# The half-GLU of the S5 branch, moved from ahead of the merge to between two branches of it

## The chip, the cores and the metric

One core of a Trainium2 chip runs the whole step in one launch. The metric is the device time in microseconds, the median of three runs. Engines: TensorE (PE; its weight loads are PEld), VectorE (DVE), ScalarE (ACT), GpSimd (POOL) and SyncE (SP, which here only issues DMAs). Each engine runs its own instructions in program order and waits on semaphores for the others.

## The reference

One inference step of a two-layer decoder trunk with model width 1024, on 1024 prompt tokens and 64 sample tokens, 1088 columns (T) in all, in float32. A layer is

```
h = rmsnorm(x);  proj = h @ w_in          # columns for four mixers, their gates z, and 4 x 1024 merge gates
y_a = conv branch          y_c = HGRN2 branch          y_d = GLA branch
sg  = gelu(y_s)                           # y_s: output of the S5 state space scan
y_b = sg * sigmoid(sg @ w_glu + b_glu) * silu(s_z)
p_b = y_b @ w_branch[b]                   # for each of the four branches, 512 -> 1024
merged = sum_b sigmoid(g_b) * p_b
x = x + merged @ w_out
```

After the second layer comes a last RMSNorm. The states of the four mixers are outputs too.

## The kernel before

Activations lie feature-major, 128 features x 1088 columns to a tile (`[128, T]`), in a pool of `NBIG = 38` such tiles. A float32 matmul is done as three passes over rounded parts: a tile is split into hi (a copy to float32r on ScalarE) and lo (a subtraction on VectorE), and hi*hi, lo*hi and hi*lo are summed in PSUM (`split`, line 1851; for weights `prep`, line 295: `whi` and `wlo`). A unit (`unit`, line 353) makes 128 output features: two halves of 544 columns, each over 4 or 8 tiles of the contraction with 3 passes and 2 matmuls of 272 columns; a unit over 4 tiles has 48 matmuls. It has three PSUM tiles (`mm`), evacuated by the function `out` that the caller gives.

All engine queues are written by one Python program, so the order of its calls is the order on each engine. Two devices put side work among a unit's matmuls. `self.defer` is a list of small jobs, of which `step` takes one at every second k of a unit (four steps to a unit over 4 tiles, eight over 8). And four lanes of generators (`rec` for the recurrences of HGRN2 and GLA, `s5l` and `tabs` for S5, `aux`) are advanced by `pump`: a bookkeeper (`Book`, line 93) holds estimated times of each engine, and a lane's next stage is written when its inputs and PSUM banks should be ready, enough tiles are free (`fits`) and VectorE is not more than `BACKLOG` = 12 us behind. `make_room` (line 234) writes lane stages at once when the pool is nearly full, `drain` (line 228) until a lane is empty.

A layer runs paired projections first (`PAIRED`), then `ORDER`: single gate units m20 to m31, the HGRN2 heads H0 to H3, the GLA pairs G0 and G1, and U. A gate unit stores sigmoid(g) to DRAM (`gsc`); silu(s_z) is in `szs`, the S5 scan's output in `vsc`, and y of each branch in `ysc`. During the last unit of G1 (line 1835) `glu_begin` loads the four S5 tiles (`yv`) and defers GELU and split of each (`xh`, `xl`). U (`glu`, line 1696) first loads y of branch 0, then for each of four units: sigmoid from PSUM (`glu`), times silu(s_z) (`sz`, loaded a unit ahead), the sum of xh and xl on POOL as the other factor, the product (`yb`, its columns reordered), and the store to `ysc`.

`merge` (line 1861) then runs 32 units, 8 for each branch in the order 0, 2, 1, 3. A unit's result is multiplied by its gate tile (`g`, loaded two units ahead with `gate`) and added to `merged` (`mg`). At d = 5 of a branch the next branch's y is loaded and its splits are deferred; ahead of branch 3 the lanes `rec` and `aux` are drained. Weights come through a ring of `RAWS` = 6 raw tiles (`w_dma`, line 273), loaded by SyncE in the order of `make_plan`. A raw load waits on SyncE until the tile that had its place has been split.

All instructions are recorded by a helper and have line 84, so the rows are told apart by their tiles.

Of the kernel before, what the change touches and what calls it, by code (L numbers as in the profile page):

```python
# [9 lines left out]
F32 = mybir.dt.float32  # L10
# [19 lines left out]

PAIRED = 'A0 M0 A1 M1 A2 M2 A3 M3 Z0 M4 Z1 M5 M6 M7 M8'
EARLY = 'm18 m19'
ORDER = 'm20 m21 m22 m23 m24 m25 m26 m27 m28 m29 m30 m31 H0 H1 H2 H3 G0 G1 U'
BRANCHES = (0, 2, 1, 3)

# [113 lines left out]
class Trunk:  # L151
# [121 lines left out]
    def w_dma(self, i):  # L273
        if i >= len(self.plan) or i in self.loaded:
            return
        self.loaded.add(i)
        self.nraw += 1
        src, M, perm = self.plan[i]
        raw = self.wp.tile([128, 4, 128], F32, tag="wraw", name=self.nm("wraw"), bufs=RAWS)
        if perm == 2:  # L280
            for k in range(4):
                self.nc.sync.dma_start(raw[:, k, :], src[128 * k:128 * k + 128, :].rearrange("(g p) m -> p g m", p=16))
        else:
            r = raw[:] if M < 256 else raw[:].rearrange("p a b -> p (a b)").rearrange("p (k m) -> p k m", m=M)
            self.nc.sync.dma_start(r, src.rearrange("(k p) m -> p k m", p=128))
        self.raws[i] = raw
# [8 lines left out]
    def prep(self, j):  # L295

        if j >= len(self.seq) or j in self.done:
            return
        self.done.add(j)
        nc = self.nc  # L300
        e, p = self.seq[j]
        perm = self.plan[e][2]
        drop = []
        for i in range(e, e + (1 if p is None else 4)):
            self.w_dma(i)
        if p is None:
            src = self.raws[e]
            drop = [e]
        else:

            a11, a21, a22, a12 = (self.raws.get(e + i) for i in range(4))
            new = lambda: self.wp.tile([128, 4, 128], F32, tag="wsum", name=self.nm("wsum"), bufs=2)
            if p == 0:
                src = a11
            elif p == 1:
                s1 = new()
                src = new()
                self.sums_[e] = s1, src
                nc.vector.tensor_add(s1[:], a21[:], a22[:])
                nc.vector.tensor_sub(src[:], s1[:], a11[:])  # L320
            elif p == 2:
                src = a12
            elif p == 3:
                src = self.sums_[e][0]
            elif p == 4:
                src = a21
                nc.vector.tensor_sub(a21[:], a11[:], a21[:])
                drop = [e, e + 1]
            elif p == 5:
                src = self.sums_.pop(e)[1]  # L330
                nc.vector.tensor_sub(src[:], a12[:], src[:])
                drop = [e + 3]
            else:
                src = a22
                drop = [e + 2]
        hi = self.wp.tile([128, 4, 128], F32R, tag="whi", name=self.nm("whi"), bufs=4)
        lo = self.wp.tile([128, 4, 128], F32R, tag="wlo", name=self.nm("wlo"), bufs=4)
        h, lv, r = hi[:], lo[:], src[:]
        if perm:
            h, lv = (x.rearrange("q k (p g) -> q k g p", g=8) for x in (h, lv))  # L340
            r = r.rearrange("q k (g p) -> q k g p", g=8)
        nc.scalar.activation(h, r, AF.Copy)
        nc.vector.tensor_sub(lv, r, h.bitcast(F32))
        for i in drop:
            self.raws.pop(i)
            self.nraw -= 1
        self.ws[j] = (hi, lo)
# [257 lines left out]
    def make_plan(self):  # L605
# [14 lines left out]
        for l in range(DEPTH):  # L620
# [13 lines left out]
            for op in ORDER.split():  # L634
                t, j = op[0], int(op[1:] or 0)
                names = []
                if t == "H":
                    names = [("c_i", j // 2, 256)] if j % 2 == 0 else []
                    names += [(n, j, 128) for n in ("c_f", "c_q", "c_z")]
                elif t == "m":  # L640
                    names = [(f"g{j // 8}", j % 8, 128)]
                elif t == "G":
                    names = [("d_q", j, 128), ("d_k", j, 128)] + ([("d_v", j, 256)] if j else [])
                    names += [("d_z", 2 * j, 128), ("d_z", 2 * j + 1, 128)]
                else:
                    add([(self.a["w_glu"][l][:, 128 * i:128 * i + 128], 128, 2) for i in range(4)])
                for n, i, M in names:
                    add(self.w_src(l, n, i, M))
            for br in BRANCHES:
                add([(self.a["w_branch"][l, br][:, 128 * d:128 * d + 128], 128, 0) for d in range(8)])  # L650

    def proj(self, l, name, j, out, last=False):
        self.unit(8, self.h, out, last)
# [1013 lines left out]
    def glu_begin(self, l):  # L1667
# [1 line left out]
        nc = self.nc  # L1669
        self.drain(self.tabs)  # L1670
        self.drain(self.s5l)
        sg = self.sg = [None] * 4

        def load(j):
            t = self.big([128, T], name="yv")
            nc.sync.dma_start(t.rearrange("q (t c) -> q t c", t=8),
                              self.vsc[l][j][:].rearrange("(t p) (g c) -> (p g) t c", t=8, g=8))
            sg[j] = t

        def act(j):  # L1680
            t = sg[j]
            nc.scalar.activation(t, t, AF.Gelu_apprx_tanh)
            hi = self.big([128, T], F32R, "xh")
            lo = self.big([128, T], F32R, "xl")
            nc.scalar.activation(hi, t, AF.Copy)
            nc.vector.tensor_sub(lo, t, hi.bitcast(F32))
            self.free(t)
            sg[j] = (hi, lo)

        for j in range(4):  # L1690
            load(j)
        self.defer += [lambda: None] * YLAG
        for j in range(4):
            self.defer.append(lambda j=j: act(j))

    def glu(self, l):
        nc = self.nc
        sg = self.sg

        def gate(j):  # L1700
            sz = self.big([128, T], name="sz")
            nc.sync.dma_start(sz, self.szs[l][j][:])
            return sz

        nxt = gate(0)
        while self.defer:
            self.defer.pop(0)()
        self.y = self.load_y(l, BRANCHES[0])
        self.defer += [lambda: None] * 4 + [lambda j=j: self.split(self.y, j) for j in range(4)]
        for j in range(4):  # L1710
            sz, nxt = nxt, gate(j + 1) if j < 3 else None
            g = self.big([128, T], name="glu")
            c = 40 + 4 * l + j
            self.unit(4, sg, self.evac(g, AF.Sigmoid, bias=self.cols[:, c:c + 1]))
            nc.vector.tensor_mul(g, g, sz)
            yt = self.big([128, T], name="yb")
            yn = yt.rearrange("p (c s) -> p s c", s=8)
            nc.gpsimd.tensor_add(sz, sg[j][0].bitcast(F32), sg[j][1].bitcast(F32))
            v3 = lambda t: t.rearrange("p (s c) -> p s c", s=8)
            nc.vector.tensor_mul(yn, v3(sz), v3(g))  # L1720
            nc.sync.dma_start(self.ysc[l][1][128 * j:128 * j + 128, :].rearrange("(g p) c -> p g c", p=16), yt)
            self.free(sz, g, yt)
        self.free(*(x for p in sg for x in p))


    def conv(self, l, j):
# [74 lines left out]
    def gla_units(self, l, pr):  # L1801
# [32 lines left out]
        for hh in range(2):  # L1834
            if pr == 1 and hh == 1:
                self.more = False
                self.glu_begin(l)
            t = self.big([128, T], name="sz")
            self.proj(l, "d_z", 2 * pr + hh, self.evac(t, AF.Silu), last=(pr == 1 and hh == 1))
            sz.append(t)  # L1840
# [20 lines left out]
    def merge(self, l):  # L1861
        nc = self.nc
        merged = [None] * 8

        units = [(n, d) for n in BRANCHES for d in range(8)]
        g = {}

        def gate(i):
# [5 lines left out]
        def branch(i, y):  # L1874
            n, d = units[i]
            gi = g.pop(i)
            first = n == BRANCHES[0]
            if first:
                merged[d] = self.big([128, T], name="mg")
            md = merged[d]  # L1880
# [14 lines left out]
        def wo_load(k):  # L1895
            self.wo[k] = self.big([128, DM], name="wo")
            nc.sync.dma_start(self.wo[k], self.a["w_out"][l][128 * k:128 * k + 128, :])

        y = self.y
        gate(0)  # L1900
        gate(1)
        while self.defer:
            self.defer.pop(0)()
        for i, (n, d) in enumerate(units):
            b = i // 8
            if d == 0 and b:
                while self.defer:
                    self.defer.pop(0)()
                y = nxt
            if d == 5 and b < 3:  # L1910
                if b == 2:
                    self.drain(self.rec)
                    self.drain(self.aux)
                nxt = self.load_y(l, BRANCHES[b + 1])
                self.defer += [lambda: None] * 4 + [lambda y=nxt, j=j: self.split(y, j) for j in range(4)]
            if b == 3:
                self.defer.append(lambda k=d: wo_load(k))
                if d > 1:
                    self.defer.append(lambda k=d - 2: self.split(self.wo, k))
                if d > 0:  # L1920
                    self.defer.append(lambda k=d - 1: self.split(merged, k))
                if d == 7:
                    self.defer.append(lambda: self.split(self.wo, 6))
            gate(i + 2)
            branch(i, y)
        while self.defer:
            self.defer.pop(0)()
        self.split(self.wo, 7)
# [109 lines left out]
    def layer(self, l):  # L2038
# [27 lines left out]
        for op in ORDER.split():  # L2066
# [2 lines left out]
                self.hgrn_units(l, i)  # L2069
            elif op[0] == "m":  # L2070
                self.gate_unit(l, i)
            elif op[0] == "G":
                self.gla_units(l, i)
            else:
                self.glu(l)
        self.merge(l)
        self.mg_h = self.mg
        self.out_proj(l)
# [42 lines left out]
```

## Time and profile before

| | us |
|---|---|
| median of 3 runs | 3140.22 (3135.49 to 3143.92) |
| the profiled execution | 3139.61 |
| its span, first to last instruction | 3137.8 |
| PE busy in it | 2998.1 |
| DVE busy in it | 1890.1 |
| ACT busy in it | 1109.5 |
| mean of a weight copy `whi<-wraw` on ACT, x400 | 0.686 |
| mean granted TensorE clock | 0.976 of full speed |

A granted clock of 1.00 is 2.4 GHz and 0.50 is 1.2 GHz. Layer 0's U and merge lie at about 1204 to 1500 us of the span, layer 1's at about 2741 to 3037. In the rows a name like `mm<-hi,whi` is output and inputs by the program's tile names. A few per cent of the matmul records are missing from the trace.

### The profile page before, as it was taken

The numbers are of one execution on the slowest core, as the hardware profiler recorded it, in microseconds if no ns is written. First come the engines' busy times: TensorE is split into PE (matmuls) and PEld (weight loads), VectorE is DVE, ScalarE is ACT, GpSimd is POOL, SyncE is SP. The second block draws the span as 40 slices with busy tenths as digits, with TensorE's granted clock in tenths as the row PEclk, the third lists the DMA queues.
The fourth block names the chain that finished last, engine by engine and source line by source line (L and its number), as shares of the span: only waits on it lengthen the run. The fifth ranks groups of instructions, "written<-read, shape, count | busy, mean of one in ns | idle before, by whom it ended". The sixth has DMA issues, their size and how long they took to land. (4 is left out here: it accounts for less than half of the span.)

```text
span 3137.8 us, 55699 instructions
## 1 busy us (share of the span) xinstructions
PE 2998.1 (96%) x23154; PEld 2901.2 (92%) x23154; DVE 1890.1 (60%) x3228; ACT 1109.5 (35%) x1881; POOL 445.4 (14%) x500
## 2 busy tenths in 40 slices
PE   8899999999999998899999999999999999979998
PEld 7899999989899997889889999999899999869997
DVE  5766654487556465677446656535877655458662
ACT  5333343223333427133333334422233334541321
POOL 2000000331101021222110000003401011112220
PEclk9899999999999999899999999999999999979999
DMA  4122234331212114445222222333221121253532
GB/s 127 49 76 83 86 96 124 107 104 57 65 49 67 32 40 144 162 142 204 95 65 76 80 88 80 94 120 114 89 65 58 50 67 35 81 159 125 189 141 87
DMA packets 281264, 296.05 MB, mean 94 GB/s; under 512 B 16288, under 2 KB 240304, under 8 KB 281012
## 3 DMA queue, kind: packets, MB, share of 16 engines
q1 hardware_dynamic: 272644, 265.37, 27.2%
q0 software_dynamic: 8368, 27.13, 2.7%
q8 instruction: 182, 2.98, 0.4%
q14 instruction: 70, 0.57, 0.1%
HBM read 208.24 MB, written 84.19 MB: 93 GB/s over the span
## 5 line engine op out<-in xcount | busy, mean ns | idle before, releaser
L84 PE MATMUL mm<-hi,whi 128*128 128x272 f32 (+1 forms) x2680 | 569.9, 293 | 48.8 <-DVE mg L84 35.9
L84 PE MATMUL mm<-hi,wlo 128*128 128x272 f32 (+1 forms) x2680 | 567.7, 293 | 0.0
L84 PE MATMUL mm<-lo,whi 128*128 128x272 f32 (+1 forms) x2680 | 567.3, 292 | 0.0
L84 DVE TENSOR_TENSOR wlo<-wraw,whi 128x512 fp32r<-128x512 f32 x400 | 303.9, 763 | 319.7 <-ACT whi L84 318.3
L84 PEld LDWEIGHTS mm<-hi,whi 128*128 128x128 f32 x2680 | 425.7, 191 | 54.2 <-DVE mg L84 35.0
L84 PEld LDWEIGHTS mm<-hi,wlo 128*128 128x128 f32 x2680 | 425.3, 191 | 3.3 <-issue 2.3
L84 PEld LDWEIGHTS mm<-lo,whi 128*128 128x128 f32 x2680 | 426.2, 191 | 0.9 <-issue 0.4
L84 PE MATMUL mm<-xh,whi 128*128 128x272 f32 (+1 forms) x1784 | 387.0, 297 | 28.7 <-ACT xh L84 15.1
L84 PE MATMUL mm<-xc,whi 128*128 128x272 f32 x2432 | 402.1, 287 | 0.0
L84 PE MATMUL mm<-xh,wlo 128*128 128x272 f32 (+1 forms) x1784 | 383.9, 295 | 8.8 <-DVE wlo L84 8.8
L84 PE MATMUL mm<-xl,whi 128*128 128x272 f32 (+1 forms) x1784 | 384.6, 296 | 3.8 <-DVE xl L84 3.8
L84 ACT ACTIVATE whi<-wraw 128x512 fp32r<-128x512 f32 x400 | 272.3, 686 | 303.7 <-PE mm L84 186.2
L84 PEld LDWEIGHTS mm<-xc,whi 128*128 128x128 f32 x2432 | 341.3, 189 | 0.0
L84 PEld LDWEIGHTS mm<-xh,whi 128*128 128x128 f32 x1784 | 287.1, 193 | 33.2 <-ACT xh L84 16.1
L84 PEld LDWEIGHTS mm<-xh,wlo 128*128 128x128 f32 x1784 | 286.9, 193 | 13.2 <-DVE wlo L84 11.4
L84 PEld LDWEIGHTS mm<-xl,whi 128*128 128x128 f32 x1784 | 287.6, 193 | 7.3 <-DVE xl L84 6.4
L84 PE MATMUL mm<-xc,wlo 128*128 128x272 f32 x1216 | 250.7, 288 | 0.0
L84 PEld LDWEIGHTS mm<-xc,wlo 128*128 128x128 f32 x1216 | 189.9, 188 | 0.0
L84 ACT ACTIVATE whi<-wsum 128x512 fp32r<-128x512 f32 x114 | 78.9, 692 | 279.6 <-DVE wsum L84 260.5
L84 DVE TENSOR_TENSOR wlo<-wsum,whi 128x512 fp32r<-128x512 f32 x114 | 85.2, 748 | 107.8 <-ACT whi L84 107.8
L84 ACT ACT_TABLE_LOAD x108 | 138.6, 1283 | 13.1 <-PE mm L84 10.7
L84 ACT ACTIVATE g<-mm 128x544 f32<-128x544 f32 x56 | 35.0, 625 | 234.8 <-PE mm L84 234.8
(374 smaller groups left out, 4857.6 us busy)
## 6 DMA issues: line engine op xcount, KB each, us to landing
wraw<-in_w_in_dram SPq DMA_DIRECT2D x328, 256.0 KB
g<-gsc SPq DMA_DIRECT2D x64, 544.0 KB
y<-ysc SPq DMA_DIRECT2D x32, 544.0 KB
wraw<-in_w_branch_dram SPq DMA_DIRECT2D x64, 256.0 KB
gsc<-g SPq DMA_DIRECT2D x28, 544.0 KB
gsc<-ga SPq DMA_DIRECT2D x18, 544.0 KB
gsc<-gb SPq DMA_DIRECT2D x18, 544.0 KB
ysc<-o POOLq DMA_DIRECT2D x16, 544.0 KB, 3.3
```

The costliest lines, as they stand in the source:

```text
L84: r = fn(*a, **kw)
```

## The change

`U` leaves `ORDER` and becomes a stage of the merge: `STAGES = '0 2 U 1 3'`. Branch 0's y is loaded during the last unit of G1, and the merge follows that unit. `glu_begin` (now also the loads of silu(s_z)) is called at d = 4 of branch 2; its deferred jobs also form gelu * silu(s_z) on VectorE (`su`). `glu` then needs one product for each unit, and its result is not stored: it is split in SBUF and used by branch 1. Its rows stay in the group order of the S5 tiles, so the rows of `w_branch[1]` are loaded in that order (perm 3), in four DMAs for a raw tile instead of one. The POOL sum, the stores to `ysc[1]` and the loads from it go.

```diff
-ORDER = 'm20 ... m31 H0 H1 H2 H3 G0 G1 U'
-BRANCHES = (0, 2, 1, 3)
+ORDER = 'm20 ... m31 H0 H1 H2 H3 G0 G1'
+STAGES = '0 2 U 1 3'
...
-        if perm == 2:
+        if perm >= 2:
             for k in range(4):
                 self.nc.sync.dma_start(raw[:, k, :], src[128 * k:128 * k + 128, :].rearrange("(g p) m -> p g m", p=16))
...
         def act(j):
-            t = sg[j]
+            t = yv[j]
+            load(j + 2)
             nc.scalar.activation(t, t, AF.Gelu_apprx_tanh)
...
             nc.vector.tensor_sub(lo, t, hi.bitcast(F32))
-            self.free(t)
-            sg[j] = (hi, lo)
+            nc.vector.tensor_mul(t, t, sz[j])
+            self.free(sz[j])
+            self.sg[j], self.su[j] = (hi, lo), t
...
     def glu(self, l):
+        y = []
+        for j in range(4):
+            g = self.big([128, T], name="glu")
+            c = 40 + 4 * l + j
+            self.unit(4, self.sg, self.evac(g, AF.Sigmoid, bias=self.cols[:, c:c + 1]), last=(j == 3))
+            yt = self.big([128, T], name="yb")
...
+            nc.vector.tensor_mul(yn, v3(self.su[j]), v3(g))
+            self.free(self.su[j], g)
+            y.append(yt)
+            if j == 3:
+                self.split(y, 3)
+            else:
+                self.defer.append(lambda j=j: self.split(y, j))
         while self.defer:
             self.defer.pop(0)()
-        self.y = self.load_y(l, BRANCHES[0])
-        self.defer += [lambda: None] * 4 + [lambda j=j: self.split(self.y, j) for j in range(4)]
-        for j in range(4):
-            sz, nxt = nxt, gate(j + 1) if j < 3 else None
...
-            nc.vector.tensor_mul(g, g, sz)
-            yt = self.big([128, T], name="yb")
-            yn = yt.rearrange("p (c s) -> p s c", s=8)
-            nc.gpsimd.tensor_add(sz, sg[j][0].bitcast(F32), sg[j][1].bitcast(F32))
...
-            nc.sync.dma_start(self.ysc[l][1][128 * j:128 * j + 128, :].rearrange("(g p) c -> p g c", p=16), yt)
+        return y
...
             if pr == 1 and hh == 1:
                 self.more = False
-                self.glu_begin(l)
+                self.y = self.load_y(l, int(STAGES[0]))
+                self.defer += [lambda: None] * 4 + [lambda j=j: self.split(self.y, j) for j in range(4)]
...
+        for b, n in enumerate(stages):
+            while self.defer:
+                self.defer.pop(0)()
+            if n == "U":
+                y = self.glu(l)
+                continue
+            y = y if y is not None else nxt
+            for d in range(8):
+                if d == (4 if stages[b + 1:][:1] == ["U"] else 5) and b + 1 < len(stages):
+                    nxt = begin(stages[b + 1])
...
+                gate(i + 2)
+                branch(i, y)
+                i += 1
+            y = None
```

## Rows read from the trace of the kernel before

**Rows 1.** The page, part 1: busy time of each engine, share of the span, instructions.
```profile
PE 2998.1 (96%) x23154; PEld 2901.2 (92%) x23154; DVE 1890.1 (60%) x3228; ACT 1109.5 (35%) x1881; POOL 445.4 (14%) x500
```
**Rows 2.** Waits of TensorE, 2715 to 2960: waiter, releaser, us in total, times, longest.
```profile
PE mm L84 <- DVE mg L84: 18.1, 2, 17.4
```
**Rows 3.** Timeline of TensorE, first branch units: start, us, instruction, count, idle and releaser.
```profile
1269.14 0.82 PE L84 MATMUL mm<-hi,whi 128*128 128x272 f32 x2 [17.17 <-DVE mg L84]
...
2807.54 0.82 PE L84 MATMUL mm<-hi,whi 128*128 128x272 f32 x2 [17.43 <-DVE mg L84]
```
**Rows 4.** Timeline of VectorE, end of U in layer 1.
```profile
2797.36 2.11 DVE L84 TENSOR_TENSOR yb<-sz,glu 128x1088 f32<-128x1088 f32 x1 [2.64 <-POOL sz L84]
2806.76 0.72 DVE L84 TENSOR_TENSOR mg<-g,mm 128x544 f32<-128x544 f32 x1 [7.29 <-DMA g<-gsc]
```
**Rows 5.** Timeline of SyncE, last GLA unit to the first branch unit of layer 1.
```profile
2733.26 16.22 SPq L84 DMA_DIRECT2D wraw<-in_w_branch_dram  x2
...
2799.50 0.53 SPq L84 DMA_DIRECT2D ysc<-yb  x1
2800.09 2.89 SPq L84 DMA_DIRECT2D g<-gsc  x3
```
**Rows 6.** Windows: stretch, us, busy us of each engine (instructions), granted clock, DMA.
```profile
2807.00:2812.00 5.00, 4.46 (x19) 4.46 (x20) 2.95 (x5) 0.00 (x0) 0.00 (x0) 0.50 0.81 280
1270.00:1400.00 130.00, 125.35 (x959) 119.97 (x959) 98.78 (x153) 36.46 (x56) 31.61 (x23) 0.96 0.43 148
1290.00:1350.00 60.00, 57.94 (x480) 55.83 (x478) 53.42 (x94) 10.51 (x17) 17.40 (x12) 1.00 0.42 144
```
**Rows 7.** Timeline of TensorE, first matmuls of U and of branch 0, layer 1.
```profile
2745.07 0.82 PE L84 MATMUL mm<-xh,whi 128*128 128x272 f32 x2 [3.62 <-ACT xh L84]
...
2780.99 0.41 PE L84 MATMUL mm<-hi,whi 128*128 128x272 f32 x2
```
**Rows 8.** Timeline of ScalarE at the start of U, layer 1.
```profile
2742.76 1.11 ACT L84 ACTIVATE yv<-yv 128x1088 f32<-128x1088 f32 x1
...
2745.03 1.28 ACT L84 ACT_TABLE_LOAD   x1
2746.33 0.62 ACT L84 ACTIVATE sz<-mm 128x544 f32<-128x544 f32 x1
```
**Rows 9.** Tile y: instruction, count, ns min/median/max, first and last start, shape.
```profile
L84 ACT ACTIVATE hi<-y x32: 1089/1112/1155, 1228.1 to 2977.5; 128x1088 fp32r<-128x1088 f32 x32
L84 DVE TENSOR_TENSOR lo<-y,hi x32: 1274/1287/2459, 1235.3 to 2982.6; 128x1088 fp32r<-128x1088 f32 x32
```
**Rows 10.** Tile glu, the same columns.
```profile
L84 ACT ACTIVATE glu<-mm,cols x16: 674/718/755, 1225.9 to 2781.2; 128x544 f32<-128x544 f32 x16
...
L84 DVE TENSOR_TENSOR yb<-sz,glu x8: 2114/2232/2367, 1233.1 to 2797.4; 128x1088 f32<-128x1088 f32 x8
```
**Rows 11.** Timeline of TensorE after a short stop in layer 0.
```profile
1398.41 0.51 PE L84 MATMUL mm<-hi,whi 128*128 128x272 f32 x2 [2.52 <-DVE g L84]
...
1400.65 0.66 PE L84 MATMUL mm<-hi,whi 128*128 128x272 f32 x2
1401.11 0.66 PE L84 MATMUL mm<-lo,whi 128*128 128x272 f32 x2
```
**Rows 12.** Windows, instructions of the tiles mm alone: PE, PEld, DVE, ACT, clock, DMA.
```profile
1270.00:1400.00 130.00, 98.53 (x704) 93.32 (x704) 20.90 (x30) 0.00 (x0) 0.96 0.43 148
1336.00:1389.00 53.00, 33.27 (x226) 30.91 (x226) 6.41 (x9) 0.00 (x0) 0.94 0.41 140
```
**Rows 13.** Timeline of SyncE: GLU weights, and one branch unit's weights.
```profile
1171.53 5.87 SPq L84 DMA_DIRECT2D wraw<-in_w_glu_dram  x8
...
1410.62 0.38 SPq L84 DMA_DIRECT2D wraw<-in_w_branch_dram  x1
```
**Rows 14.** Timeline of TensorE: two successive sums of the last recurrence, layer 0.
```profile
1226.12 0.62 PE L84 MATMUL sm<-prh,ones_r 128*128 128x512 f32 x2
...
1278.19 0.20 PE L84 MATMUL sm<-prh,ones_r 128*64 128x64 f32 x1
```

More of the change, by code (lines that the diff above doesn't have):

```diff
@@ L32 @@
 EARLY = 'm18 m19'
-ORDER = 'm20 m21 m22 m23 m24 m25 m26 m27 m28 m29 m30 m31 H0 H1 H2 H3 G0 G1 U'
-BRANCHES = (0, 2, 1, 3)
+ORDER = 'm20 m21 m22 m23 m24 m25 m26 m27 m28 m29 m30 m31 H0 H1 H2 H3 G0 G1'
+STAGES = '0 2 U 1 3'
 TAILT = 5
@@ L338, in prep @@
         h, lv, r = hi[:], lo[:], src[:]
-        if perm:
+        if perm in (1, 2):
             h, lv = (x.rearrange("q k (p g) -> q k g p", g=8) for x in (h, lv))
@@ L645, in make_plan @@
                 else:
-                    add([(self.a["w_glu"][l][:, 128 * i:128 * i + 128], 128, 2) for i in range(4)])
+                    raise ValueError(op)
                 for n, i, M in names:
                     add(self.w_src(l, n, i, M))
-            for br in BRANCHES:
-                add([(self.a["w_branch"][l, br][:, 128 * d:128 * d + 128], 128, 0) for d in range(8)])
+            for s in STAGES.split():
+                if s == "U":
+                    add([(self.a["w_glu"][l][:, 128 * i:128 * i + 128], 128, 2) for i in range(4)])
+                else:
+                    add([(self.a["w_branch"][l, int(s)][:, 128 * d:128 * d + 128], 128, 3 * (s == "1"))
+                         for d in range(8)])
     def proj(self, l, name, j, out, last=False):
@@ L1671, in glu_begin @@
         self.drain(self.s5l)
-        sg = self.sg = [None] * 4
+        self.sg, self.su = [None] * 4, [None] * 4
+        yv, sz = [None] * 4, [None] * 4
+        for j in range(4):
+            yv[j] = self.big([128, T], name="yv")
+            nc.sync.dma_start(yv[j].rearrange("q (t c) -> q t c", t=8),
+                              self.vsc[l][j][:].rearrange("(t p) (g c) -> (p g) t c", t=8, g=8))
         def load(j):
[L1675 to L1678, printed above, removed]
+            if j < 4:
+                sz[j] = self.big([128, T], name="sz")
+                nc.sync.dma_start(sz[j], self.szs[l][j][:])
         def act(j):
-            t = sg[j]
+            t = yv[j]
+            load(j + 2)
             nc.scalar.activation(t, t, AF.Gelu_apprx_tanh)
@@ L1686, in act @@
             nc.vector.tensor_sub(lo, t, hi.bitcast(F32))
-            self.free(t)
-            sg[j] = (hi, lo)
-        for j in range(4):
-            load(j)
+            nc.vector.tensor_mul(t, t, sz[j])
+            self.free(sz[j])
+            self.sg[j], self.su[j] = (hi, lo), t
+        load(0)
+        load(1)
         self.defer += [lambda: None] * YLAG
@@ L1697, in glu @@
         nc = self.nc
[L1698 to L1705, printed above, removed]
+        y = []
+        for j in range(4):
+            g = self.big([128, T], name="glu")
+            c = 40 + 4 * l + j
+            self.unit(4, self.sg, self.evac(g, AF.Sigmoid, bias=self.cols[:, c:c + 1]), last=(j == 3))
+            yt = self.big([128, T], name="yb")
+            yn = yt.rearrange("p (c s) -> p s c", s=8)
+            v3 = lambda t: t.rearrange("p (s c) -> p s c", s=8)
+            nc.vector.tensor_mul(yn, v3(self.su[j]), v3(g))
[3 more added lines that the diff above has]
+                self.split(y, 3)
+            else:
+                self.defer.append(lambda j=j: self.split(y, j))
         while self.defer:
             self.defer.pop(0)()
-        self.y = self.load_y(l, BRANCHES[0])
-        self.defer += [lambda: None] * 4 + [lambda j=j: self.split(self.y, j) for j in range(4)]
-        for j in range(4):
-            sz, nxt = nxt, gate(j + 1) if j < 3 else None
-            g = self.big([128, T], name="glu")
-            c = 40 + 4 * l + j
-            self.unit(4, sg, self.evac(g, AF.Sigmoid, bias=self.cols[:, c:c + 1]))
-            nc.vector.tensor_mul(g, g, sz)
-            yt = self.big([128, T], name="yb")
-            yn = yt.rearrange("p (c s) -> p s c", s=8)
-            nc.gpsimd.tensor_add(sz, sg[j][0].bitcast(F32), sg[j][1].bitcast(F32))
-            v3 = lambda t: t.rearrange("p (s c) -> p s c", s=8)
-            nc.vector.tensor_mul(yn, v3(sz), v3(g))
-            nc.sync.dma_start(self.ysc[l][1][128 * j:128 * j + 128, :].rearrange("(g p) c -> p g c", p=16), yt)
-            self.free(sz, g, yt)
-        self.free(*(x for p in sg for x in p))
+        return y
     def conv(self, l, j):
@@ L1863, in merge @@
         merged = [None] * 8
-        units = [(n, d) for n in BRANCHES for d in range(8)]
+        stages = [x if x == "U" else int(x) for x in STAGES.split()]
+        units = [(n, d) for n in stages if n != "U" for d in range(8)]
         g = {}
@@ L1876, in branch @@
             gi = g.pop(i)
-            first = n == BRANCHES[0]
+            first = n == stages[0]
             if first:
@@ L1897, in wo_load, with begin @@
             nc.sync.dma_start(self.wo[k], self.a["w_out"][l][128 * k:128 * k + 128, :])
+        def begin(s):
+            if s == "U":
+                self.glu_begin(l)
+                return None
+            if s == 3:
+                self.drain(self.rec)
+                self.drain(self.aux)
+            y = self.load_y(l, s)
+            self.defer += [lambda: None] * 4 + [lambda j=j: self.split(y, j) for j in range(4)]
+            return y
         y = self.y
@@ L1901, in merge @@
         gate(1)
[L1902 to L1925, printed above, removed]
+        i = 0
+        for b, n in enumerate(stages):
[8 more added lines that the diff above has]
+                    nxt = begin(stages[b + 1])
+                if b + 1 == len(stages):
+                    self.defer.append(lambda k=d: wo_load(k))
+                    if d > 1:
+                        self.defer.append(lambda k=d - 2: self.split(self.wo, k))
+                    if d > 0:
+                        self.defer.append(lambda k=d - 1: self.split(merged, k))
+                    if d == 7:
+                        self.defer.append(lambda: self.split(self.wo, 6))
+                gate(i + 2)
+                branch(i, y)
+                i += 1
+            y = None
         while self.defer:
@@ L2071, in layer @@
                 self.gate_unit(l, i)
-            elif op[0] == "G":
+            else:
                 self.gla_units(l, i)
-            else:
-                self.glu(l)
         self.merge(l)
```

## The prediction

> **What bounds the kernel now.** I read first the page's table of engines: TensorE is busy 96% of the span, VectorE 60%, ScalarE 35% [rows 1]. The end moves only by what TensorE does in its missing 4%, or by making it do more; the change leaves its matmuls as they are. So next I listed TensorE's waits from the last GLA unit of layer 1 to the end of the branches: two waits of 18.1 us in all, nearly all of it in one of 17.43 us, and its twin of 17.17 us in layer 0 [rows 2, 3]. Then the other queues at that place. VectorE finishes the last product of the U stage at 2799.5 and then stands until 2806.76 for the gate tile of the first branch unit [rows 4]. SyncE says why so late: its four stores of U's result and its loads of silu(z) stand in program order ahead of the gate loads, so the gate loads go out only at 2800.09, behind the store of the last tile [rows 5]. The cause is thus a chain of silu(z) load, product, POOL sum, product, store, gate load; TensorE has filled its three PSUM tiles meanwhile and stops. Behind the stop its clock is granted at 0.50, the 1.2 GHz level [rows 6].
>
> The second loss is at U's start. TensorE ends the last GLA unit at 2741.3, gets the first GELU tile at 2745.07 and begins the first branch unit at 2780.99 [rows 7]. U is 4 units of 48 matmuls. Pairs run 0.25 us apart at full clock, 0.1255 us a matmul, so 24.1 us and 0.5 for one pair of the recurrence: of the 39.7 us 15.1 are waiting and half clock. ScalarE makes that wait: after the gate exponentials it loads tables and alternates GELU, copy and the SiLU of the projection [rows 8].
>
> **The change part by part, per layer.** (a) The stop of 17.3 us goes (mean of both layers). The gate loads are now issued at the merge's start behind the y loads and two weight loads; no store or POOL sum is ahead. With it go about 2.0 us of half clock: in the 5 us behind the stop 4.46 us of matmuls ran at half speed [rows 6]. Together 19.3. What is late next there is the split of branch 0's y.
>
> (b) U's start becomes branch 0's start. ScalarE's queue is then the gate exponentials (till 2741.5: the first GELU starts at 2742.76, behind a table load), one table load of 1.28, the SiLU 0.62, a weight copy 0.69 (the page's mean) and four copies of 1.11; three table loads and four GELUs of 1.11 are gone from here [rows 8, 9]. The first copy ends near 2745.1, the same as the GELU tile's now, the others 1.1 us after each other. TensorE waits 3.8 us, then 0.9 for the first low part, and the rest keeps pace at half clock (a k-tile of 6 matmuls takes 1.36 us, a low part 1.29). With some 3 us for the clock I take 7.7 of loss against 15.1: 7.4 saved. Bounds: nothing saved if ScalarE is fed later than I place it, 15.1 if the splits end before the GLA unit does. The four y loads take the place in SyncE's program that the four loads of GELU inputs have now, so they aren't later.
> A switch of tables costs 1.28 us on ScalarE and 1.30 from its start to the next function's [rows 8]. The Trainium skill (ScalarE: Activation LUTs, "What ACT_TABLE_LOAD costs") puts a drain of about 1.38 us on top, 2.66 in all. By that, three switches fewer would give 4.1 us more per layer and 3094; the trace shows no such drain, and the row decides.
>
> (c) A new stop stands between U and branch 1, because the last result tile is made and split right before it is used: Sigmoid 0.72, product 2.23, copy 1.11, low part 1.29 [rows 9, 10]. With 0.3 of hand-offs the high part is there 4.35 us after U's last matmul; three finished k-tiles cover 18 matmuls, 2.26 us, so 2.1 idle, and 1.05 more for the low part. A stop of 2.52 us today is followed by pairs 0.45 apart instead of 0.25 for about 4.4 us [rows 11], 1.8 lost. I take 5.0. Bounds: 0 where matmuls of the recurrence fill it, 7.2 without the cover. Queued behind on ScalarE are only weight copies that are two units ahead. What no longer stands here, or at branch 1's load, are four stores and four loads of 544 KB and four POOL sums; they are off TensorE's path except through (a), so they count nothing more.
>
> (d) VectorE in branches 0 and 2. From 1270 to 1400 it is busy 98.8 of 130 us, TensorE 125.35 [rows 6], so TensorE idles 4.65. Afterwards these 16 units share VectorE with more: the first products of the last recurrence and the first gate products (about 9 us, now in U's time), branch 0's splits (5.2), eight GELU-phase operations of 1.29 (10.3), less branch 1's splits (5.6): 118 us. TensorE's own need there: 16 units, 96.4 us, plus the recurrence's. The latter is 125.35 less 704 recorded branch matmuls of 0.1255 (88.4), 37, of which some 2 are clock: 131 in all [rows 6, 12]. VectorE must then be 90% dense. Its densest stretch of this mixture, 1290 to 1350, is 53.4 of 60, 0.89 [rows 6]: 133 us, 2 idle. The mean of the whole stretch, 0.76, gives 155, 24 idle. The dense row is the nearer one, since TensorE is not the cause of the gaps in it; but the GELU operations come in a burst (10.3 us in two units of 6), so I take 8 idle, 3 more than now. Bounds: 4.7 gained, 19.4 lost.
>
> (e) Branch 1's weights come in four DMAs of 64 KB a unit instead of one: the GLU weights come so today, at 5.87/8 = 0.73 us each with waits, against 0.38 [rows 13]. A unit needs 2.9 us, and about 1 for its gate tile (2.89 for three, [rows 5]), of the unit's 6.0: hidden, cost 0; uncovered it would be 8 units of 2.5, 20 us.
>
> Sum per layer: 19.3 + 7.4 - 5.0 - 3 = 18.7; two layers 37.4. The profiled execution took 3139.61 (span 3137.8 and 1.8 around it), 0.6 below the median of the runs, 3140.22. So 3139.6 - 37.4 = 3102.
>
> **The rivals.**
> E, all of (d) dissolves and (c) keeps its clock: 19.3 + 7.4 + 4.65 - 3.2 = 28.1, 3083. For it: the last recurrence now makes no headway in U, one sum at 1226.12 and the next at 1278.19 [rows 14], and will move on at once. Against it: the GELU burst.
> B, VectorE paces branches 0 and 2 at 0.76: 19.3 + 7.4 - 5.0 - 19.4 = 2.3, 3135, no change. For it: 118 of 131 us; against it: the dense row.
> C, the gate tile is late again, since SyncE also waits up to 16 us at a weight tile before it [rows 5]: half of the stop stays, 18.7 - 8.7 = 10, 3120. Against it: the PSUM tiles cover three half-units.
> D, branch 1's weights are late: 18.7 - 20, 3142. The Trainium skill (SBUF — State Buffer, "The DMA setup-cost knee") speaks for D: about 2 us for every DMA whatever its size, so coalesce; 24 more would be an estimated 48 us a layer if none overlapped, 3198. In the trace TensorE waits for no GLU weight inside U.
> A, slower: SBUF room. The code counts live tiles against 38 and, when full, stages the recurrence at once, whether its inputs are ready or not. At the fourth GELU tile 32 are taken (8 sums, 8 y, 3 gates, 12 GELU tiles, 1 silu), so the recurrence may hold 5 or 6; in mid-course it holds 8. If it stands at its last level when asked (1335.8 today), it runs bare to its end at 1389: the 226 branch matmuls that now lie among it, 28.3 us [rows 12], are then not there to cover it. 18.7 - 28.3 = -9.6 a layer, 3159. It decides from a stall of 23 us. Against it: the recurrence loses U's 4 units before branch 0 but also the 5 units in which it stood [rows 14], so it should be in its last norm by then.
>
> **How the numbers follow.** My forecast 3102 has 0.53, with 3088 to 3118 as its own range; E 0.14, B 0.14, C 0.08, A 0.08, D 0.03. 0.3% is 9.4 us, about what a measurement of this kernel can tell from no change. Faster: forecast, E, C and 0.03 of B, 0.78. Same: the rest of B, 0.02 of D and 0.01 of A, 0.14. Slower: 0.08. A range from 3082 to 3138 leaves out A, half of E and a little of B and D.
>
> **What would show it.** Right: no TensorE wait over 10 us at a branch's first unit; TensorE idle 4 to 5 us before branch 0 and about 3 before branch 1, with 0.50 of clock behind each; no POOL operation in U; VectorE 0.85 to 0.9 busy through branches 0 and 2. Wrong: a wait for the first gate product (C), long runs of recurrence matmuls without branch matmuls among them in branch 2's second half (A), waits for gate products through branch 2 (B), or for weight parts in branch 1 (D).

## The result, and the profile after

The changed kernel takes 3108.1 us (median of four runs, 3107.03 to 3110.55) against 3140.26 for the kernel before beside it: ratio 0.990, 95% interval 0.9882 to 0.9917, 32 us less. 3102 was predicted. The profiled execution of after took 3107.93, its span 3106.2, 31.6 less than the span before, at a mean granted clock of 0.982 (before 0.976).

The page of after, part 1, beside [rows 1]: TensorE's busy time is the same to 2 us, so nearly all of the 31.6 us is idle time.
```profile
PE 2996.3 (96%) x23154; PEld 2900.6 (93%) x23154; DVE 1885.7 (61%) x3228; ACT 1102.4 (35%) x1876; POOL 429.0 (14%) x492
```
Waits of TensorE in after, 2715 to 2960 (waiter, releaser, us in total, times, longest), beside [rows 2]. The wait of 17.43 us for `mg` is gone; in its place stand waits of at most 3.5, for split tiles (`hi`, `lo`) and for gate products (`g`).
```profile
PE mm L84 <- DVE g L84: 6.7, 3, 2.9
PE mm L84 <- ACT hi L84: 6.5, 2, 3.5
...
```
The timeline of TensorE in after places them. The first two lines are sums of the last recurrence in layer 0, now 7 us apart (52 in [rows 14]). Then follow, in layer 1: branch 0's start (beside [rows 7]), the longest wait for a gate product in branch 0 (0.89, beside the 17.43 of [rows 3]), three waits in branch 2, and branch 1's start behind U.
```profile
1219.30 0.62 PE L84 MATMUL sm<-prh,ones_r 128*128 128x512 f32 x2
...
1226.28 0.19 PE L84 MATMUL sm<-prh,ones_r 128*64 128x64 f32 x1
...
2731.02 0.82 PE L84 MATMUL mm<-hi,whi 128*128 128x272 f32 x2 [3.51 <-ACT hi L84]
2732.34 0.82 PE L84 MATMUL mm<-lo,whi 128*128 128x272 f32 x2 [0.51 <-DVE lo L84]
...
2761.05 0.49 PE L84 MATMUL mm<-hi,whi 128*128 128x272 f32 x2 [0.89 <-DVE mg L84]
...
2858.84 0.51 PE L84 MATMUL mm<-hi,whi 128*128 128x272 f32 x2 [2.91 <-DVE g L84]
...
2865.29 0.52 PE L84 MATMUL mm<-hi,whi 128*128 128x272 f32 x2 [1.69 <-DVE g L84]
...
2870.67 0.48 PE L84 MATMUL mm<-hi,whi 128*128 128x272 f32 x2 [2.10 <-DVE g L84]
...
2907.18 0.52 PE L84 MATMUL mm<-hi,whi 128*128 128x272 f32 x2 [3.01 <-ACT hi L84]
2908.51 0.82 PE L84 MATMUL mm<-lo,whi 128*128 128x272 f32 x2 [0.81 <-DVE lo L84]
```
ScalarE in after at branch 0's start, beside [rows 8]: one table load between the gate exponential and the SiLU, then all four copies in a row, no GELU.
```profile
2726.40 1.11 ACT L84 ACTIVATE f<-f 128x1088 f32<-128x1088 f32 x1
2727.53 1.28 ACT L84 ACT_TABLE_LOAD   x1
2728.82 0.62 ACT L84 ACTIVATE sz<-mm 128x544 f32<-128x544 f32 x1
...
2729.86 4.10 ACT L84 ACTIVATE hi<-y 128x1088 fp32r<-128x1088 f32 x4
```
SyncE in after, beside [rows 5] and [rows 13]: the gate loads go out at 2731.20, as branch 0 begins and 12 us before VectorE first uses one (2743.43); branch 1's weights take 2.47 us of issue a unit.
```profile
2718.49 12.61 SPq L84 DMA_DIRECT2D wraw<-in_w_branch_dram  x2
2731.20 1.39 SPq L84 DMA_DIRECT2D g<-gsc  x3
...
2853.40 2.47 SPq L84 DMA_DIRECT2D wraw<-in_w_branch_dram  x4
```
VectorE in after, in the burst of GELU jobs, where TensorE waits for `g` in branch 2. It stands 2.17 us for ScalarE's first `xh`, while the gate product stands behind in its queue; from 2859.46 on two more jobs of the burst, four operations of 1.28 to 1.29, stand ahead of the gate product of 2864.52.
```profile
2855.53 1.29 DVE L84 TENSOR_TENSOR xl<-yv,xh 128x1088 fp32r<-128x1088 f32 x1 [2.17 <-ACT xh L84]
2856.86 1.29 DVE L84 TENSOR_TENSOR yv<-yv,sz 128x1088 f32<-128x1088 f32 x1
2858.07 0.71 DVE L84 TENSOR_TENSOR g<-g,mm 128x544 f32<-128x544 f32 x1
...
2863.31 1.29 DVE L84 TENSOR_TENSOR yv<-yv,sz 128x1088 f32<-128x1088 f32 x1
2864.52 0.71 DVE L84 TENSOR_TENSOR g<-g,mm 128x544 f32<-128x544 f32 x1
```
Windows of after (columns as in [rows 6]): branches 0 and 2 of layer 1, the burst in branch 2, the first 5 us of branch 0 and of branch 1.
```profile
2731.00:2882.00 151.00, 141.47 (x1060) 135.09 (x1061) 118.55 (x174) 49.53 (x70) 34.20 (x22) 0.95 0.48 154
2853.00:2873.00 20.00, 13.30 (x91) 12.58 (x90) 17.63 (x18) 13.25 (x13) 4.42 (x2) 0.91 0.64 225
...
2731.00:2736.00 5.00, 4.47 (x18) 4.16 (x19) 5.00 (x5) 3.48 (x4) 0.00 (x0) 0.50 0.80 257
...
2907.00:2912.00 5.00, 4.01 (x20) 3.79 (x20) 2.61 (x3) 0.65 (x2) 1.37 (x1) 0.66 0.12 47
```

### The profile page after: what moved, and what is told of

The parts are those of the page before. It is cut to its first block, busy times and chain, and to the rows that moved or that the text cites. A ratio compares the mean times of both kernels' runs of the same rounds, so it can differ in the third digit from the quotient of the medians.

```text
span 3106.2 us, 55696 instructions
## 1 busy us (share of the span) xinstructions
PE 2996.3 (96%) x23154; PEld 2900.6 (93%) x23154; DVE 1885.7 (61%) x3228; ACT 1102.4 (35%) x1876; POOL 429.0 (14%) x492
## 4 chain that ended last, share of the span: by engine, by line
PE 87%; DVE 7%; ACT 3%; issue 2%; DMA 1%; SPq 0%; POOL 0%; DVEq 0%; POOLq 0%; ACTq 0%
PE mm L84 75%; PE sm L84 12%; DVE H L84 1%; ACT L84 1%; DVE wlo L84 1%; DVE w L84 1%; ACT whi L84 0%; DVE yb L84 0%; ACT hi L84 0%; DVE pr L84 0%; DVE lo L84 0%; DVE att L84 0%; ACT sz L84 0%; ACT osq L84 0%; DVE xl L84 0%
## 5 line engine op out<-in xcount | busy, mean ns | idle before, releaser
L84 PEld LDWEIGHTS mm<-xh,whi 128*128 128x128 f32 x1784 | 284.8, 191 | 17.1 <-ACT whi L84 9.4
L84 POOL TENSOR_TENSOR mg<-mg,g 128x544 f32<-128x544 f32 x48 | 90.4, 1884 | 256.6 <-DVE g L84 243.2
```

The source lines that it names most:

```text
L84: r = fn(*a, **kw)
```

## The experiments

Times are medians. "Before" beside them was 3138.42 (runs 1 to 4), 3138.11 (5 to 8) and 3137.72 (9 to 12); ratios are to it.

### What the old stop was made of (1, 2, 5, 9: the kernel before, with U in its old place)

**1. Gates first.** 3120.0, ratio 0.9941 (0.9926 to 0.9956).
In `glu`, behind `load_y`:
```diff
+        for i in range(2):
+            self.g[i] = self.big([128, T], name="g")
+            nc.sync.dma_start(self.g[i], self.gsc[l][BRANCHES[0]][128 * i:128 * i + 128, :])
```


> The kernel before, with one move: the first two gate tiles are loaded at U's start instead of behind U's four stores. Nothing else changes: U stands ahead of branch 0, and the DRAM round trip of its result and the POOL sums stay. Theory (order: the change gained by taking gate loads and products out from behind U's chain): the gate load's 7.2 us leave each stop of 17.3, but VectorE still reaches the first gate product only when U's last product ends (2799.5 in the profile of before), so some 10 us of each stop stay: 14 us less, 3126. Rival (traffic: the change gained by the 16 transfers and 8 POOL sums that it saved): nothing was saved here, so 3140.

18 us less. But a stop stays, and it still waits for `mg`:
```profile
1262.12 0.82 PE L84 MATMUL mm<-hi,whi 128*128 128x272 f32 x2 [9.51 <-DVE mg L84]
```
So the late gate load, which the prediction took for the end of the whole chain, accounts for 7.7 of 17.2 us as long as the rest is there.

**2. Gates and all four silu(z) tiles first.** 3118.17, 0.9936 (0.9921 to 0.9951).
```diff
-        nxt = gate(0)
+        szs = [gate(j) for j in range(4)]
```


> As the run above, and all four silu(z) tiles of U are loaded at its start instead of one ahead of each unit, so no product of U waits behind a store on SyncE. Theory (order): VectorE's chain ends at about 2789 to 2792 in the time of before, when TensorE has just filled its three PSUM tiles; the stop shrinks to 0 to 3 us: 15 to 19 us a layer less, 3102 to 3110, as fast as the changed kernel although U stays where it was and its result goes through DRAM. Rival (traffic): 3140, or 3126 at the best.

A miss: 9.44 us of stop stay in layer 1. The timelines of VectorE and POOL in this run say why. Each product `yb` waits 2.7 us for the POOL sum, the chain is late by the end of U, and the branch product `mg` is the next instruction behind it. POOL could not start the sum sooner, since the program writes it over the silu(z) tile (`sz`) that the product before it (`glu`) still reads:
```profile
2775.25 1.28 DVE L84 TENSOR_TENSOR glu<-glu,sz 128x1088 f32<-128x1088 f32 x1
...
2776.66 2.53 POOL L84 TENSOR_TENSOR sz<-xh,xl 128x1088 f32<-128x1088 f32 x1 [4.20 <-DVE glu L84]
...
2779.22 2.12 DVE L84 TENSOR_TENSOR yb<-sz,glu 128x1088 f32<-128x1088 f32 x1 [2.70 <-POOL sz L84]
...
2785.70 2.12 DVE L84 TENSOR_TENSOR yb<-sz,glu 128x1088 f32<-128x1088 f32 x1 [2.64 <-POOL sz L84]
2787.65 0.71 DVE L84 TENSOR_TENSOR mg<-g,mm 128x544 f32<-128x544 f32 x1
```
No run gives the sum a tile of its own, so that it could run while U's matmuls do; whether that alone would have removed the stop stays open.

**5. Gates first, and no POOL sum:** gelu * silu(z) formed in the GELU jobs as in the changed kernel, U where it was, its result still stored and loaded. 3086.06, 0.9839 (0.9824 to 0.9853).
```diff
+            nc.vector.tensor_mul(t, t, sz[j])
...
-            nc.vector.tensor_mul(g, g, sz)
-            nc.gpsimd.tensor_add(sz, sg[j][0].bitcast(F32), sg[j][1].bitcast(F32))
-            nc.vector.tensor_mul(yn, v3(sz), v3(g))
+            nc.vector.tensor_mul(yn, v3(self.su[j]), v3(g))
```


> The kernel before, with U in its old place and its result stored to and loaded from DRAM as before, but with the gate tiles loaded at U's start and without the POOL sums: gelu * silu(z) is formed in the GELU jobs, and one VectorE product a unit is left. The run with silu(z) loaded first kept a stop of 9.5 us; in its trace VectorE stands 2.7 us in each unit for the POOL sum, 10.7 in four. Theory (VectorE's order behind the POOL sum): those 10.7 us go, and with them the rest of the stop: 36 to 40 us less than before, 3099 to 3104, with no move and with all 16 transfers. Rival (the move or the saved transfers were needed): the stop stays near 9.5 us, 3118 to 3120.

The stop is gone, and the run is 13 us faster than expected and 22 faster than the changed kernel: with the sums gone and the gates early, the move of U costs time. Two things leave U here, the wait for each POOL sum and the product with silu(z), 1.28 us of VectorE a unit, and no run takes them out one by one. TensorE's timeline: U still begins with the old wait of 3.62, but the last recurrence's sums now follow each other inside U (before: one, then none for 52 us, [rows 14]):
```profile
2738.47 0.62 PE L84 MATMUL sm<-prh,ones_r 128*128 128x512 f32 x2
2747.71 0.20 PE L84 MATMUL sm<-prh,ones_r 128*64 128x64 f32 x1
...
2765.37 0.52 PE L84 MATMUL mm<-hi,whi 128*128 128x272 f32 x2 [1.07 <-DVE mg L84]
```
The branches are shorter too: from the end of the stop to the first split of `merged` (`hi<-mg`) layer 0 takes 1253.24 to 1427.7, 174.5 us, against 1269.14 to 1455.8, 186.7, before. The windows of this run and of before, in this order (columns as in [rows 6]), show the same matmuls to within 6 records; TensorE idles 0.6 us instead of 4.7, runs at full clock, and VectorE has 9.7 us less to do there:
```profile
1253.24:1427.70 174.46, 173.85 (x1392) 169.83 (x1393) 122.70 (x185) 44.49 (x67) 45.90 (x31) 1.00 0.51 172
...
1269.14:1455.80 186.66, 182.00 (x1398) 176.63 (x1399) 132.39 (x196) 45.80 (x69) 48.61 (x32) 0.96 0.47 163
```

**9. As 5, gates late as before.** 3092.85, 0.9861 (0.9846 to 0.9876). The diff is 5's without that of 1.

> The kernel before, with U in its old place and its result stored and loaded again, the gate product formed among the GELU jobs and no POOL sum; the first two gate tiles are loaded where they were, behind U's stores. Theory (the old stop is two parts in a row: about 9.7 us for VectorE standing in order behind four POOL sums, about 7.6 us for the gate load behind the last store): only the first part goes, about 15 us more than the run with both removed (3086), so 3101 (3096 to 3106), with a stop of 6 to 8 us at the first branch unit. Rival (one cause, the gate load was late only because VectorE was): 3084 to 3090 and no stop over 2 us.

A miss of my theory: the stop is 1.52 and 2.08 us, not 6 to 8. The rival has the stop nearly right, its time is missed by 3 us.
```profile
2771.29 0.52 PE L84 MATMUL mm<-hi,whi 128*128 128x272 f32 x2 [2.08 <-DVE mg L84]
```
So the two parts don't simply add: without the POOL sums U's stores go out early enough that the gate load behind them is nearly in time (VectorE waits 0.81 us for it in layer 1). Taking the sums out, with the silu(z) product moved, is worth 45 us, the gates alone 18, both 52. Of the 6.8 us between 5 and 9, 1.8 are idle by the listed waits; where the other 5 are stays open.

### The waits in the changed kernel (3, 4, 6, 8, 11)

**3. GELU jobs spread**, two empty jobs between them. 3107.39, 0.9901 (0.9887 to 0.9916).
```diff
-            self.defer.append(lambda j=j: act(j))
+            self.defer += [lambda: None] * (2 if j else 0) + [lambda j=j: act(j)]
```


> The changed kernel, with two empty jobs between the four GELU jobs: they lie over three units and a step of branch 2 instead of over one unit and a step. Same instructions. Theory (burst): TensorE's waits for gate products there (6.1 us in layer 0, 6.7 in layer 1, and about 2 each of half clock) come from three jobs of 2.2 us ScalarE and 2.6 us VectorE in one unit of 6; spread out, 5 to 7 us a layer go: 3094 to 3098. Rival (density: VectorE is as a whole too full through branches 0 and 2): the wait moves with the jobs, 3105 to 3110.

A miss: the waits only moved (2.21, 0.40 and 4.61 for `g` in layer 1), and the time lies in the rival's range. ScalarE's timeline in this run shows the price: the last norm's functions now fall between the GELUs, and each change of function loads a table, six loads in 15 us:
```profile
2855.23 1.28 ACT L84 ACT_TABLE_LOAD   x1
2856.53 1.12 ACT L84 ACTIVATE yv<-yv 128x1088 f32<-128x1088 f32 x1
2857.68 1.11 ACT L84 ACTIVATE xh<-yv 128x1088 fp32r<-128x1088 f32 x1
2858.80 1.28 ACT L84 ACT_TABLE_LOAD   x1
2860.10 1.05 ACT L84 ACTIVATE osq<-sm,epsc 128x384 f32<-128x384 f32 x2
...
2862.18 1.28 ACT L84 ACT_TABLE_LOAD   x1
```
**6. GELU one unit later**, one empty job between. 3112.05, 0.9916 (0.9901 to 0.9931).
```diff
-                if d == (4 if stages[b + 1:][:1] == ["U"] else 5) and b + 1 < len(stages):
+                if d == 5 and b + 1 < len(stages):
...
-            self.defer.append(lambda j=j: act(j))
+            self.defer += [lambda: None] * int(j > 0) + [lambda j=j: act(j)]
```


> The changed kernel, with U's loads at d = 5 instead of 4 and one empty job between GELU jobs, so that the first GELU is written about one unit later, behind the last norm of the recurrence. Theory (ScalarE's order: VectorE stands in order for a GELU that is queued among the norm's functions; spreading the jobs put three more table switches between them): the norm goes first, the waits of 6.1 and 6.7 us there fall to 2 to 3: 3098 to 3102. Rival (density of VectorE): the waits only move, 3105 to 3110.

A miss again: one long wait stands in place of the three, still in branch 2 (6.39 us in layer 1, 6.59 in layer 0). The S5 tiles were loaded a unit later too, and now the load is late: ScalarE waits 3.73 us for it, and VectorE, with a gate product behind in its queue, 5.88 for the copy.
```profile
2870.44 0.79 PE L84 MATMUL mm<-hi,whi 128*128 128x272 f32 x2 [6.39 <-ACT xh L84]
...
2861.58 1.28 ACT L84 ACT_TABLE_LOAD   x1 [3.73 <-DMA yv<-vsc]
...
2865.16 1.29 DVE L84 TENSOR_TENSOR xl<-yv,xh 128x1088 fp32r<-128x1088 f32 x1 [5.88 <-ACT xh L84]
```
So this run doesn't tell what the later place alone is worth. Of 3 and 6 neither gains.

**4. U ahead of branch 2's last unit.** 3100.59, 0.9879 (0.9862 to 0.9895), 7.5 less than the changed kernel. In this run that unit and U's four take their weights in the old order, so they multiply each other's weights, of the same shapes.
```diff
+                if d == 7 and stages[b + 1:][:1] == ["U"]:
+                    while self.defer:
+                        self.defer.pop(0)()
+                    yu = self.glu(l)
```


> The changed kernel, with U's four units ahead of the eighth unit of branch 2 instead of behind it, so that this unit stands between U's last tile and branch 1. Same instructions. Theory: the stop of 3.8 us before branch 1 and its 1.6 to 2.1 us of half clock are hidden under 6 us of matmuls: 5.5 us a layer, 3097. Rival (room: the 8 y tiles of branch 2 stay taken through U, so lane stages are written early and TensorE waits for them): 3108 or slower.

The stop ahead of branch 1 goes, as expected, but the gain is 3.75 us a layer and not 5.5: new waits of 0.67 and 1.41 for sigmoid (`glu`) appear in U, and the burst stays (2.90, 3.21).

**8. Branch 0's y one unit earlier.** 3086.47, 0.9838 (0.9824 to 0.9853), 21.6 less than the changed kernel.
```diff
-            if pr == 1 and hh == 1:
+            if pr == 1 and hh == 0:
                 self.y = self.load_y(l, int(STAGES[0]))
...
```


> The changed kernel, with branch 0's y loaded and split during the last unit but one of the GLA pair instead of the last. Same instructions. Theory: the start of branch 0 waits only because the copies stand behind the gate exponentials on ScalarE; a unit earlier they stand ahead of them, and 4.0 to 4.3 us of wait and 3 of half clock go: 7 a layer, 3094. Rival: ScalarE is full there, the copies delay the exponentials and the projections' SiLU, and TensorE waits for those: 3105 to 3112.

More than expected. Branch 0 begins without a wait for a split (the first wait is 0.52, for `mg`), and the waits for `g` shrink too. The pool is nearly full there, and `make_room` now writes six recurrence stages a layer at once, five of them in branch 2, at the price of the wait for `sql` below. They lie among the GELU jobs: the four GELUs start at 2817.24, 2819.40, 2835.53 and 2849.41, where the changed kernel has them in one burst from 2853.24 to 2860.63, and the recurrence's last sum stands at 2858.51, ahead of U (2880.30 in the changed kernel, as U runs). How much of the gain comes from this is not told apart from the early splits.
```profile
2837.57 0.44 PE L84 MATMUL sm<-sql,ones_r 128*128 128x384 f32 x1 [2.21 <-DVE sql L84]
...
2851.20 0.49 PE L84 MATMUL mm<-hi,whi 128*128 128x272 f32 x2 [0.89 <-DVE g L84]
...
2856.50 0.52 PE L84 MATMUL mm<-hi,whi 128*128 128x272 f32 x2 [1.36 <-DVE g L84]
```
**11. 8 and 4 together**, the weights in the new order. 3079.49, 0.9815 (0.98 to 0.9829), the fastest version.

> The changed kernel with branch 0's y one unit earlier (alone 3086) and U ahead of branch 2's last unit (alone 7.5 us less). This run computes the same as the reference. Theory (the two stops are separate): 3079 (3075 to 3084). Rival (VectorE then is the bound of branches 0 and 2, and what is saved at the stops is lost in the burst): 3086 to 3092.

The edits are those of 8 and 4. As the theory said: 28.6 less than the changed kernel, 7.0 less than 8 alone; the two stops are separate.

### Traffic, DMA counts, room (7, 12, 10)

**7. The transfers put back:** the changed kernel also stores U's result and loads it again into tiles that nobody reads. 3107.71, 0.9899 (0.9882 to 0.9915).
```diff
+            nc.sync.dma_start(self.ysc[l][1][128 * j:128 * j + 128, :], yt)
...
+        self.free(*self.load_y(l, 1))
```


> The changed kernel, with each result tile of U also stored to DRAM and the four tiles loaded again behind U, into tiles that nobody reads: 16 transfers of 544 KB more, all other work the same. Theory: they lie beside TensorE's work and cost nothing, 3106 to 3111, unless SyncE's loads come late behind them. Rival (traffic: half or more of the gain was the transfers saved): 3115 or slower.

As expected: the bytes that are saved by keeping the result in SBUF gain nothing that can be measured.

**12. All branch weights in quarters.** 3126.96, 0.9966 (0.9953 to 0.9979), 19 slower than the changed kernel.
```diff
+        if perm == 4:
+            for k in range(4):
+                self.nc.sync.dma_start(raw[:, k, :], src[128 * k:128 * k + 128, :])
```


> The changed kernel with the weights of all four branches loaded in four DMAs of 64 KB a unit, not only those of branch 1: 24 units a layer more. Theory (2.5 us of issue for each unit lies beside 6 us of matmuls): 3106 to 3110, no wait of TensorE for weights. Rival (SyncE's extra 1.9 to 2.5 us a unit come through, since gate tiles and y loads share its queue): 45 to 60 us a layer, over 3195; in part, over 3115.

The time missed the theory and lies where the rival had it, over 3115; yet of the theory's mechanism the part on weights held. TensorE's waits for weight parts in the whole run are those of the changed kernel (`wlo` 19.9 and 19.9, `whi` 17.1 and 16.8). What is new are waits inside the last recurrence, as branch 0 runs:
```profile
2789.80 0.47 PE L84 MATMUL sm<-prs,ones_r 128*128 128x512 f32 x1 [4.34 <-DVE prs L84]
```
The rival's late loads show on ScalarE alone: in 2700 to 3010 it waits 9.1 us for y (7.7 in the changed kernel) and 6.2 for one branch weight, while TensorE's waits for the copies (`hi`) fall from 13.0 to 11.1 in the whole run. The queue orders of the two programs differ there. `Book` counts 0.45 us of SyncE for each DMA start, and as this program is written, `make_room` writes 13 lane stages a layer at once in branches 0 and 2; for the changed kernel none. That the 19 us come from those stages alone is argued from this, not shown.

**10. As 5, GELU tiles one GLA unit earlier.** 3140.0, 1.0008 (0.9999 to 1.0018).
```diff
-            if pr == 1 and hh == 1:
+            if pr == 1 and hh == 0:
                 self.glu_begin(l)
```


> The run without POOL sum and with gates first (3086), with the S5 tiles loaded and their GELU and splits queued one GLA unit earlier. Theory (U's start loses 15 us a layer because ScalarE gets the GELUs only with the last unit; an earlier load cured branch 0's start in the changed kernel): 12 us a layer less, 3062 (3055 to 3070). Rival (no room: the 12 tiles and the recurrence do not fit in 38, lane stages are written at once and run bare): 3086 or slower.

54 us slower than 5. U's start no longer waits for `xh`, but `make_room` writes 17 stages a layer at once, and the recurrence runs bare. TensorE, and the window over it (columns as in [rows 6]):
```profile
2740.76 0.63 PE L84 MATMUL sm<-r,wgk 48*128 48x320 f32 x1 [7.75 <-DVE m L84]
...
2750.66 0.80 PE L84 MATMUL sm<-prh,ones_r 128*128 128x512 f32 x1 [9.26 <-DVE prh L84]
```
```profile
2722.00:2770.00 48.00, 13.28 (x41) 8.63 (x41) 31.21 (x38) 34.60 (x37) 2.54 (x2) 0.60 0.23 84
```
This is rival A's mechanism, at a place where the pool is fuller: 48 us with TensorE busy for 13.

## Why the prediction was right, term by term

Per layer, idle time from TensorE's timeline, and "slow" the time by which pairs of branch or U matmuls are over 0.25 us apart without a wait:

| term | predicted | layer 0 | layer 1 |
|---|---|---|---|
| (a) old stop and its half clock | +19.3 | +19.2 | +19.4 |
| (b) U's start becomes branch 0's | 15.1 - 7.7 = +7.4 | 14.2 - 7.4 = +6.8 | 15.1 - 7.2 = +7.9 |
| (c) new stop ahead of branch 1 | -5.0 | 3.82 + 2.1 = -5.9 | 3.82 + 1.6 = -5.4 |
| (d) branches 0 and 2 | -3 | -5.4 | -4.6 |
| (e) quarter loads | 0 | 0 | 0 |

That is 14.7 and 17.3, 32.0 in all; the spans differ by 31.6. (Counted from the end of the last GLA unit to the first split of `merged`, after is 15.4 and 17.7 shorter.) The forecast had 37.4; of the 5.4 between, 4.0 are the size of (d) and 1.3 that of (c).

(a) Right in size and in the remedy, wrong in its inside. I put the whole stop on the gate load at the end of a chain with silu(z) at its head. Run 2 shows that the silu(z) loads are worth 1.8 us in both layers together, run 1 that 9.5 us of stop stay without the late gate load, and run 9 that the gate load is late mostly because the stores behind the products are. What is left is the work on VectorE in U, where it stands 10.7 us for four POOL sums (run 2) and spends 5.1 on four products with silu(z). Runs 5 and 9 take out both, so the sums' part is read from the trace: their 10.7 us alone exceed the 9.4 us of stop.

(b) Right by its steps: table load, SiLU, weight copy, four copies in 4.10 us, in that order; the first wait 3.51 against 3.8, the low part 0.51 to 0.78 against 0.9, the clock at 0.50. The table load took 1.28 us and the SiLU began 1.29 behind its start. The Trainium skill (ScalarE: Activation LUTs, "What ACT_TABLE_LOAD costs") with 2.66 for a switch would have given an estimated 3094; the run does not bear that out.

(c) The cover was as taken, 18 matmuls, but the chain was longer: idle 3.01 before the high part where 2.1 stood, 0.81 for the low part against 1.05. The high part is there 5.3 us after U's last matmul in layer 1 (2901.84 to 2907.13), not 4.35. I had looked at what is queued behind on ScalarE, not at what stands ahead there: the copy of the tile before, the Sigmoid of the first half and a weight copy, so the last Sigmoid starts 1.2 us after that matmul.
```profile
2900.91 1.11 ACT L84 ACTIVATE hi<-yb 128x1088 fp32r<-128x1088 f32 x1 [2.52 <-issue]
...
2903.05 0.70 ACT L84 ACTIVATE glu<-mm,cols 128x544 f32<-128x544 f32 x1
2906.02 1.11 ACT L84 ACTIVATE hi<-yb 128x1088 fp32r<-128x1088 f32 x1 [2.27 <-DVE yb L84]
```

(d) Here the argument fails, and that its number is near is in part luck. VectorE's work was well placed (118 forecast; 118.55 in the window that also holds U's first 5 us), but I judged by its density, 0.85 to 0.9 through both branches, and it is 0.79. TensorE's long waits stand in the burst alone, where VectorE is busy 17.63 of 20 us: it stands for ScalarE's first GELU copy with a gate product queued behind it, and then has two more GELU jobs ahead of the next one. I named the burst and took 3 us for it; it costs about 5. Nothing in rows of before shows this order: it is read from the list of deferred jobs and the trace of after. Runs 3 and 6, meant to test it, don't settle it: the waits moved with the jobs.

(e) Right: no wait for weights in branch 1. By the Trainium skill (SBUF — State Buffer, "The DMA setup-cost knee") the 24 extra DMAs were an estimated 48 us a layer if none overlapped; the trace has 2.47 us of issue for four, beside a unit, and no wait. Run 12 agrees for the other branches as to weights.

The rivals: E was half right, since the recurrence does move on at once ([rows 14] against 1219.30 and 1226.28), but (d) did not dissolve. Run 5 shows a layer in which no burst follows. B came in part: its sign, waits for gate products in branch 2, is there (6.1 and 6.7 us), but in the burst alone. C and D did not occur. A did not here (`make_room` writes no stage in the merge of the changed kernel); run 10 shows that it is real.

## What to carry to other kernels

In run 2 four products that waited on VectorE for POOL, 10.7 us in all, held every product behind them in its queue: look for the product behind the wait, not only for the transfer that lands last, and take a slow helper (here a POOL sum with 2.7 us of standing for each product) out before moving a whole stage, and look first whether it starts late only because it writes over a tile that is still read. Prepare the first operands of a stage one unit earlier, and first count the free tiles that this takes: a step of this kind gained 21.6 us in one place (4 tiles) and lost 54 in another (12 tiles). Judge a burst of side jobs by what stands between two consecutive products of the main stream, not by the mean density of the engine.

## What the runs showed that I had not expected

The move that the change is about was not what gained: with U in its old place, and only the sums taken out and the gates loaded first, the kernel is 22 us faster than with the move (run 5). Spreading jobs of one function on ScalarE can cost as much as it frees: six table loads of 1.28 us in 15 us in run 3, where the changed kernel had two in 18, and no gain. And one early load that takes about 7.3 us of waiting and half clock a layer from branch 0's start gave 10.8 a layer (run 8), with the GELU jobs spread as a side effect of the fuller pool.
